# The router's second sum in another PSUM bank, and the normed rows of two latent tiles behind the choice

## The chip, the cores and the metric

The kernel runs on one core of one Trainium2 chip. The time is the device time of one execution in microseconds (us); of several executions the median is taken.

## The reference

Two layers of a transformer-like block over 1024 latent tokens and 256 context tokens of 1024 channels. Each layer mixes tokens with three parallel head groups (latent attention, a convolution module, a Hyena), and then does, for latent and context tokens apart:

```python
y = concat([rmsnorm(att, g_att), rmsnorm(conv, g_conv), rmsnorm(hy, g_hy)])   # 512 + 256 + 256 channels
x = x + g1 * (y @ w_out)
h = rmsnorm(x, norm2_g) * (1 + sc2) + sh2
# expert choice: 16 experts
aff = softmax(h @ router_w)                      # tokens x 16
gates, idx = top_k(aff.T, 2 * n_tokens // 16)    # 128 latent, 32 context tokens for each expert
y = (silu(h[idx] @ w_gate) * (h[idx] @ w_up)) @ w_down
x = x + g2 * scatter_add(idx, y * gates)
```

In layer 1, the last, only latent tokens go through this part. After it comes a final RMSNorm.

## The kernel before

The change lies in the output projection (`wout`) and at the start of the experts (`moe`) that follow it. Before them stand the input projection and the three head groups, behind them sixteen experts for each layer.

`wout(l)` works on tiles of 128 tokens: in layer 0 eight latent tiles (0 to 7) and two of context (8, 9) in the order 0, 1, 2, 3, 8, 9, 4, 5, 6, 7; in layer 1 the tiles 0 to 7. The loop calls `heads(i)` for a tile and then `channels` for the tile two places later in the order. The products use three matmuls for each block (`mm3`, lines 95 to 97: high by high, high by low, low by high).

- `channels(i)` computes the convolution's and the Hyena's share of the projection: 24 matmuls into four banks, which ScalarE (L1129) and VectorE (L1130) empty with the RMSNorm scales of the two groups. For tiles 8 and 9 two of the four products go to the "tp" banks.
- `heads(i)` computes attention's share (24 matmuls into two banks). For each half of 512 channels VectorE scales and adds (L1148), multiplies by the gate (L1149) and adds the residual stream (L1150): this is x(i). ScalarE squares and sums x (L1155), GpSimd makes the RMSNorm factor r of it. TensorE transposes x in two halves into "tp" (L1162), ScalarE copies them (L1163), 16 matmuls with the router's weights give partial logits in a bank "rt"; VectorE copies these (L1169), one further product with `sel` (the router's second sum, `pl2`) adds the parts up, and VectorE reads it into the logits "lg" (L1173). Last come the normed rows of the tile, four VectorE operations (L1181, L1182 twice each) and their write to memory `hd` from SP's queue.
- `scales(...)` makes the RMSNorm factors of the groups: matmuls with a column of ones into the bank "st", a VectorE read (L1105), and two GpSimd operations (L105, L106). Both `heads` and `channels` call it, `channels` before its products, `heads` before its own.

PSUM's eight banks in this stage are tp 2, mm 4, rt 1, st 1. `ps("st")` asks for the next use of such a bank.

After context's second tile, `route_ctx` makes context's choice (through two tiles in the bank "rt", the last one read at L1280). After tile 7, `route` makes the latent choice: softmax, and a chain of VectorE operations that sorts, ending with the copy of L1346. `moe` then loads weights, builds for the first expert the list of context tokens, gathers their rows (`fetch_ctx`, L1409), transposes them (`tokens_ctx`) and multiplies by its weights (`up_ctx`, 64 matmuls into "cx"), and does the same for latent tokens (`fetch`, `tokens`, `up`, matmuls into "acc").

The order of work on each engine's queue is made when the kernel is built: a planner with a timeline simulation takes, among the instructions that are ready, the one with the highest priority. Priority is the order of the program, unless a block raises it (`high_priority(n)`). Each engine then runs its queue in that fixed order.

Of the kernel before, what the change touches and what calls it, by code (L numbers as in the profile page):

```python
# [51 lines left out]
class Kernel:  # L52
# [988 lines left out]
    def wout(self, l, R):  # L1041
# [4 lines left out]
        with ExitStack() as es:  # L1046
# [10 lines left out]
            ps = self.banks(es, tp=2, mm=4, rt=1, st=1) if last else self.banks(es, tp=2, mm=4, rt=1, st=1)  # L1057
# [75 lines left out]
            def heads(i):  # L1133

                s = int(i >= 8)
                c = 128 * i % W
                t, y = T[i], Y[128 * i - c]
                r = scales(y[2], c, (0,))
                x = row()
                if l == 0:  # L1140
                    src = A["x"][128 * i:128 * i + 128] if not s else A["ctx"][128 * (i - 8):128 * (i - 8) + 128]
                else:
                    src = self.stream(0, i)
                nc.sync.dma_start(x, src)
                for c2 in range(2):
                    d = slice(512 * c2, 512 * c2 + 512)
                    p = product(y, 0, c, d)
                    V.scalar_tensor_tensor(t[:, d], p, r, t[:, d], ALU.mult, ALU.add)  # L1148
                    V.tensor_tensor(t[:, d], t[:, d], rows[2, s][:, d], ALU.mult)  # L1149
                    V.tensor_tensor(x[:, d], t[:, d], x[:, d], ALU.add)  # L1150
                nc.sync.dma_start(self.stream(l, i), x)
                h = self.t(PX, [128, 1024], F32, "h2")
                s1 = self.t(PX, [128, 1], F32, "s1")
                r1 = self.t(PX, [128, 1], F32, "r1")
                S.activation(h, x, AF.Square, scale=1.0 / 32, accum_out=s1)  # L1155
                R["normed"] = self.rsqrt(r1, s1)

                hT = self.t(PX, [128, 8, 128], F32, "h2T")
                for b in range(2):
                    p = ps("tp", (128, 4, 128))  # L1160
                    for k in range(4):
                        self.T.transpose(p[:, k, :], x[:, 128 * (4 * b + k):128 * (4 * b + k) + 128], self.ident)  # L1162
                    S.activation(hT[:, 4 * b:4 * b + 4, :], p, AF.Copy)  # L1163
                pl = ps("rt")
                for k in range(8):
                    j = k % 4
                    self.mm(pl[32 * j:32 * j + 32, 0:128], rw[:, k, :], hT[:, k, :], k < 4, k >= 4)
                lp = self.t(PX, [128, 128], F32, "lpart")
                V.tensor_copy(lp, pl[:, 0:128])  # L1169
                pl2 = ps("rt")  # L1170
                self.mm(pl2[:, 0:32], lp, sel)
                e = slice(16 * s, 16 * s + 16)
                V.scalar_tensor_tensor(R["lg"][:, i, :], pl2[:, e], r1, cst[:, e], ALU.mult, ALU.add)  # L1173
                if i == 7:
                    return lambda: normed(i, s, h, x, r1)
                normed(i, s, h, x, r1)

            def normed(i, s, h, x, r1):
                for b in range(2):
                    d = slice(512 * b, 512 * b + 512)  # L1180
                    V.scalar_tensor_tensor(h[:, d], x[:, d], r1, rows[4, s][:, d], ALU.mult, ALU.mult)  # L1181
                    V.tensor_tensor(h[:, d], h[:, d], rows[3, s][:, d], ALU.add)  # L1182
                nc.sync.dma_start(self.hd[l][128 * i:128 * i + 128], h)

            def router():

                n = 1 if last else 2
                rr = self.t(PX, [128, 8, 16], F32, "rr", bufs=1)
                rc = self.t(PX, [128, 2, 2, 8], F32, "rc", bufs=1)
                rs = self.t(PX, [128, 32], F32, "rsum", bufs=1)  # L1190
                nc.sync.dma_start(rr, A["router_w"][l])
                nc.sync.dma_start(sel, A["k_sel"])
                for j, v in enumerate((4, 3)):
                    for s in range(n):
                        nc.sync.dma_start(rc[:, j, s], self.modd[l][v, s].rearrange("(k p) -> p k", p=128))
                if last:
                    G.memset(rw, 0.0)
                    G.memset(rs, 0.0)
                for s in range(n):
                    e = slice(16 * s, 16 * s + 16)  # L1200
                    G.tensor_tensor(rw[:, :, e], rr, rc[:, 0, s].unsqueeze(2).to_broadcast([128, 8, 16]), ALU.mult)
                    tmp = self.t(PX, [128, 8, 16], F32, "rtmp", bufs=1)
                    G.tensor_tensor(tmp, rr, rc[:, 1, s].unsqueeze(2).to_broadcast([128, 8, 16]), ALU.mult)
                    V.tensor_reduce(rs[:, e], tmp.rearrange("p k e -> p e k"), AX.X, ALU.add)
                p = ps("rt")
                self.mm(p[:, 0:32], self.ones[:, 0:1].to_broadcast([128, 128]), rs)
                V.tensor_copy(cst, p[:, 0:32])
# [8 lines left out]
            for s in range(1 if last else 2):  # L1216
                for v in (2, 4, 3):
                    r = self.t(PX, [128, 1024], F32, f"row{v}_{s}", bufs=1)
                    (G if last else nc.sync).dma_start(r, _bc(self.modd[l][v, s], 128))
                    rows[v, s] = r  # L1220
            router()
            order = list(range(8)) if last else [0, 1, 2, 3, 8, 9, 4, 5, 6, 7]
            for n, i in enumerate(order):
                end = heads(i)
                if i == 7:
                    self.route(R, ps, "mm" if last else "tp", row() if last else self.t(PX, [128, 1024], F32, "ro", bufs=1))
                    end()
                if n + 2 < nt:
                    channels(order[n + 2])
                if i == 9:  # L1230
                    ar, wk = (self.t(PX, [16, 256], F32, n, bufs=1) for n in ("arc", "wkc"))
                    self.route_ctx(R, ps, ar, wk)
# [116 lines left out]
    def moe(self, l, R):  # L1349
        nc, A, S, V, G = self.nc, self.A, self.S, self.V, self.G  # L1350
        last = l == 1
        with ExitStack() as es:
# [38 lines left out]
            def fetch_ctx(e):  # L1391
                d = E[e]
                p = ps("dt")
                ohc = self.t(P, [128, 2, 64], F32R, "ohc", bufs=1)
                for q in range(2):
                    V.tensor_tensor(ohc[:, :, 32 * q:32 * q + 32], iota[:, 0:32].unsqueeze(1).to_broadcast([128, 2, 32]),
                                    R["slot"][:, 8:10, e:e + 1].to_broadcast([128, 2, 32]), ALU.is_equal)
                for i in range(2):
                    self.mm(p[0:64, 4:8], ohc[:, i, :], R["rhs"][:, 8 + i, e, :], i == 0, i == 1)
                idc = self.t(P, [64, 1], U32, "idc", bufs=4)  # L1400
                V.tensor_copy(idc, p[0:64, 4:5])
                d["idc2"] = self.t(P, [64, 1], U32, "idc2", bufs=6)
                V.scalar_tensor_tensor(d["idc2"], p[0:64, 4:5], 2.0, half, ALU.mult, ALU.add)
                glc = self.t(P, [64, 2], F32, "glc", bufs=4)
                V.tensor_copy(glc, p[0:64, 6:8])
                d["gatec"] = self.t(P, [64, 1], F32, "gatec", bufs=6)
                G.tensor_tensor(d["gatec"], glc[:, 0:1], glc[:, 1:2], ALU.add)
                d["xgc"] = self.t(P, [32, 1024], F32, "xgc", bufs=1)
                G.indirect_dma_start(d["xgc"], None, self.hd[l], bass.IndirectOffsetOnAxis(ap=idc[0:32, :], axis=0))  # L1409
# [15 lines left out]
            def tokens_ctx(e):  # L1425
                d = E[e]
                d["xc"] = self.t(P, [128, 8, 32], F32, "xcT")
                p = ps("dt")
                for k in range(8):
                    self.T.transpose(p[:, 32 * k:32 * k + 32], d["xgc"].rearrange("p (f k) -> p k f", k=8)[:, k, :], self.ident[0:32, 0:32])  # L1430
                S.activation(d["xc"].rearrange("p a b -> p (a b)"), p[:, 0:256], AF.Copy)
# [40 lines left out]
            def up_ctx(e, kh):  # L1472
                d = E[e]
                if kh == 0:
                    d["pc"] = ps("cx")
                for kk in range(4):
                    k = 4 * kh + kk
                    for m in range(2):
                        for c in range(2):
                            r = 32 * (2 * m + c)  # L1480
                            self.mm(d["pc"][r:r + 32, :], d["xc"][:, k, :], raw(e, m, kh)[:, kk, 512 * c:512 * c + 512], k == 0, k == 7)
# [92 lines left out]
                E[0]["raw"] += [weights(nm, 0, 1) for nm in ("w_gate", "w_up")]  # L1574
            if not last:
                E[0]["raw"] += [weights(nm, 0, 1) for nm in ("w_gate", "w_up")]
                fetch_ctx(0)
                tokens_ctx(0)
                up_ctx(0, 0)
                up_ctx(0, 1)  # L1580
            fetch(0)
            tokens(0)
            for e in range(1, AHEAD):
# [244 lines left out]
```

## Time and profile before

| | before |
|---|---|
| median of three runs | 3397.47 us (3392.35 to 3399.98) |
| the profiled execution's own time | 3397.73 us |
| its span | 3395.9 us |
| its mean granted TensorE clock | 0.954 of full speed |
| TensorE matmul busy | 3123.1 us (92%) |
| TensorE weight load busy (beside matmuls) | 2226.8 us (66%) |
| VectorE busy | 2531.3 us (75%) |
| ScalarE busy | 1690.2 us (50%) |
| GpSimd busy | 1295.2 us (38%) |
| DMA | 660.84 MB, mean 195 GB/s |

The time is the median over executions; the rows further down come from one profiled execution, whose span is what the profiler saw from the first instruction to the last. Busy shares are averages over the whole span, with stages in it that differ. [...]

### The profile page before, as it was taken

How to read it: one execution, taken by the hardware profiler on the slowest of the kernel's cores; microseconds unless marked ns; L12 is line 12 of the kernel's file. 1: busy time of each engine (PE TensorE's matmuls, PEld its weight loads, DVE VectorE, ACT ScalarE, POOL GpSimd, SP SyncE). 2: the span in 40 equal slices, each digit the busy share in tenths (PEclk: the TensorE clock that was granted, in tenths of full speed). 3: DMA queues.
4: the chain of work that ended last, by engine and by line, in shares of the span. 5: the costliest groups of instructions: out<-in, count | busy, mean ns of one | idle time of the engine just before them, and what ended most of it. 6: DMA issues, size and time to landing. Idle time of an engine off the chain costs nothing. (4 is left out here: it accounts for less than half of the span.)

```text
span 3395.9 us, 42767 instructions
## 1 busy us (share of the span) xinstructions
PE 3123.1 (92%) x15607; PEld 2226.8 (66%) x15607; DVE 2531.3 (75%) x3520; ACT 1690.2 (50%) x2447; POOL 1295.2 (38%) x1128
## 2 busy tenths in 40 slices
PE   8898989999999599999999969899998959999996
PEld 2467865666567376666666657656664747888885
DVE  7755698777657677777777656977775769998986
ACT  4315235433443256656565543353434427777775
POOL 4421255754653212112221122565557423433334
PEclk9898989999999799999999979899999969999998
DMA  8881112231253567777777631221233469999994
GB/s 306 323 279 53 38 64 82 54 104 43 73 162 116 209 241 289 278 286 279 290 292 274 225 101 44 81 72 51 69 110 99 149 235 347 378 382 372 382 378 176
DMA packets 142523, 660.84 MB, mean 195 GB/s; under 512 B 24712, under 2 KB 63272, under 8 KB 111593
## 3 DMA queue, kind: packets, MB, share of 16 engines
q1 hardware_dynamic: 117129, 582.89, 45.6%
q0 software_dynamic: 24768, 74.05, 7.9%
q8 instruction: 123, 2.02, 0.2%
q10 hardware_dynamic: 416, 1.18, 0.1%
q14 instruction: 87, 0.71, 0.1%
HBM read 589.28 MB, written 68.78 MB: 194 GB/s over the span
## 5 line engine op out<-in xcount | busy, mean ns | idle before, releaser
L91 DVE TENSOR_TENSOR mwl<-raw,mwh 128x1024 fp32r<-128x1024 f32 x710 | 881.5, 1278 | 217.5 <-ACT mwh L90 207.2
L90 ACT ACTIVATE mwh<-raw 128x1024 fp32r<-128x1024 f32 x768 | 791.8, 1057 | 350.5 <-PE acc L97 118.1
L96 PE MATMUL acc<-mwl,xh 128*128 128x512 f32 x1024 | 405.0, 396 | 0.0
L97 PE MATMUL acc<-mwh,xl 128*128 128x512 f32 x1024 | 403.0, 396 | 0.1
L95 PE MATMUL acc<-mwh,xh 128*128 128x512 f32 x1024 | 373.7, 401 | 6.0 <-ACT xh L90 6.0
L803 POOL TENSOR_TENSOR psum<-psum,pt 128x512 f32<-128x512 f32 x252 | 332.3, 1338 | 66.7 <-ACT pt L788 56.8
L788 ACT ACTIVATE pt<-s 128x512 f32<-128x512 f32 (+1 forms) x336 | 195.9, 586 | 257.4 <-PE s L97 220.8
L1528 POOL DMA_INDIRECT xd<-ymoe,idx x31 | 113.4, 3656 | 541.6 <-DVE ymoe L1524 465.1
L758 DVE TENSOR_REDUCE mx<-p 128x1 f32<-128x512 f32 (+1 forms) x374 | 206.0, 585 | 70.0 <-PE p L100 68.9
L95 PEld LDWEIGHTS acc<-mwh,xh 128*128 128x128 f32 x1024 | 192.4, 189 | 68.6 <-ACT mwh L90 10.9
L96 PEld LDWEIGHTS acc<-mwl,xh 128*128 128x128 f32 x1024 | 193.9, 189 | 40.1 <-DVE mwl L91 0.8
L91 POOL TENSOR_TENSOR mwl<-raw,mwh 128x1024 fp32r<-128x1024 f32 x58 | 150.1, 2592 | 181.3 <-ACT mwh L90 117.5
L97 PEld LDWEIGHTS acc<-mwh,xl 128*128 128x128 f32 x1024 | 192.8, 189 | 39.1 <-DVE xl L91 0.6
L100 PE MATMUL o<-pt,Vt 128*64 128x512 f32 (+1 forms) x672 | 184.7, 613 | 0.0
L564 DVE SCALAR_TENSOR_TENSOR cacc<-pad,cw,cacc 128x1295 f32<-128x1295 f32 (+1 forms) x90 | 165.8, 1842 | 1.3
L97 PE MATMUL mm<-hTh,wfl 128*128 128x512 f32 (+1 forms) x400 | 151.3, 379 | 12.8 <-DVE wfl L91 12.8
L95 PE MATMUL mm<-hTh,wfh 128*128 128x512 f32 (+1 forms) x400 | 152.5, 381 | 4.0 <-ACT wfh L90 4.0
L96 PE MATMUL mm<-hTl,wfh 128*128 128x512 f32 (+1 forms) x400 | 152.0, 380 | 0.0
L562 POOL TENSOR_TENSOR cacc<-cacc,tap 128x1295 f32<-128x1295 f32 (+1 forms) x30 | 97.0, 3233 | 120.7 <-ACT tap L561 118.5
L100 PE MATMUL cx<-raw,xcT 128*32 128x512 f32 x1024 | 123.7, 607 | 0.0
L95 PE MATMUL mm<-woh,yhh 128*128 128x512 f32 x280 | 115.7, 416 | 8.5 <-ACT wt L1129 4.4
L96 PE MATMUL mm<-wol,yhh 128*128 128x512 f32 x280 | 111.9, 400 | 0.1
(546 smaller groups left out, 7228.9 us busy)
## 6 DMA issues: line engine op xcount, KB each, us to landing
raw<-in_w_gate_dram SPq DMA_DIRECT2D x64, 2048.0 KB
raw<-in_w_up_dram SPq DMA_DIRECT2D x64, 2048.0 KB
raw<-in_w_down_dram SPq DMA_DIRECT2D x64, 2048.0 KB
mw<-in_mod_w_dram SPq DMA_DIRECT2D x48, 1024.0 KB
ht<-in_k_C_dram POOLq DMA_DIRECT2D x24, 512.0 KB, 5.1
wfr<-in_w_fm_dram SPq DMA_DIRECT2D x20, 512.0 KB
hd<-h SPq DMA_DIRECT2D x18, 512.0 KB
fw<-in_k_filt_dram POOLq DMA_DIRECT2D x17, 512.0 KB, 5.8
```

Source lines behind the costliest of these rows:

```text
L90: self.S.activation(hi, src, AF.Copy)
L91: (eng or self.V).tensor_tensor(lo, src, hi.bitcast(F32), ALU.subtract)
L95: mm(out, ah, bh, start=first, stop=False, skip_group_check=True)
L96: mm(out, ah, bl, start=False, stop=False, skip_group_check=True)
L97: return mm(out, al, bh, start=False, stop=last, skip_group_check=True)
L100: return self.T.matmul(out, a, b, start=first, stop=last, skip_group_check=True)
L562: G.tensor_tensor(a, a, t, ALU.add)
L564: V.scalar_tensor_tensor(a, x, w2[:, ct, k:k + 1], a, ALU.mult, ALU.add)
L758: V.tensor_reduce(mx[:, q, n:n + 1], p[:, :N], AX.X, ALU.max)
L788: S.activation(pt[:, :N], p[:, :N], AF.Exp, scale=ATT_SCALE)
L803: (V if tail and n > 8 else G).tensor_tensor(sm[:, :N], st.sums[i][:, :N], pt[:, :N], ALU.add)
L1528: G.indirect_dma_start(self.xd[l], bass.IndirectOffsetOnAxis(ap=d["idx"], axis=0), y, None, compute_op=ALU.add)
```

## The change

There are three edits. The router's second sum asks for the bank "st" instead of "rt". The normed rows of tile 6, and not only those of tile 7, come behind the latent choice in the program's order; a list keeps what has to be made there. And in layer 0 the first expert's context work (list and gather, transposes, 64 matmuls) stands in a block of raised priority, so that the planner places it up to 2500 places earlier than the program's order.

```diff
                 V.tensor_copy(lp, pl[:, 0:128])
-                pl2 = ps("rt")
+                pl2 = ps("st")
                 self.mm(pl2[:, 0:32], lp, sel)
                 e = slice(16 * s, 16 * s + 16)
                 V.scalar_tensor_tensor(R["lg"][:, i, :], pl2[:, e], r1, cst[:, e], ALU.mult, ALU.add)
-                if i == 7:
-                    return lambda: normed(i, s, h, x, r1)
-                normed(i, s, h, x, r1)
+                if i in (6, 7):
+
+                    ends.append(lambda: normed(i, s, h, x, r1))
+                else:
+                    normed(i, s, h, x, r1)
...
             router()
+            ends = []
             order = list(range(8)) if last else [0, 1, 2, 3, 8, 9, 4, 5, 6, 7]
             for n, i in enumerate(order):
-                end = heads(i)
+                heads(i)
                 if i == 7:
                     self.route(R, ps, "mm" if last else "tp", row() if last else self.t(PX, [128, 1024], F32, "ro", bufs=1))
-                    end()
+                    for end in ends:
+                        end()
...
             if not last:
                 E[0]["raw"] += [weights(nm, 0, 1) for nm in ("w_gate", "w_up")]
-                fetch_ctx(0)
-                tokens_ctx(0)
-                up_ctx(0, 0)
-                up_ctx(0, 1)
+                with self.tc.high_priority(2500):
+                    fetch_ctx(0)
+                    tokens_ctx(0)
+                    up_ctx(0, 0)
+                    up_ctx(0, 1)
```

## Rows read from the trace of the kernel before

**Rows 1.** Window of layer 0's projection; columns: stretch, length, PE, PEld, DVE, ACT, POOL busy (instructions), granted clock, DMA share, GB/s.

```profile
1000.00:1107.00 107.00, 107.00 (x598) 84.96 (x597) 84.91 (x155) 38.95 (x65) 42.03 (x59) 1.00 0.35 125
```

**Rows 2.** Windows of tile st alone, layer 0 and layer 1; busy columns PE, PEld, DVE, POOL.

```profile
1007.70:1091.00 83.30, 4.67 (x36) 5.87 (x37) 1.79 (x12) 6.79 (x12) 1.00 0.36 127
2662.30:2690.10 27.80, 1.57 (x12) 1.89 (x13) 0.59 (x4) 2.25 (x4) 1.00 0.44 152
```

**Rows 3.** Timeline of tp in layer 0 (start, us, instruction), then the window of tile mm.

```profile
1015.16 0.60 ACT L1163 ACTIVATE h2T<-tp 128x512 f32<-128x512 f32 x1 [0.48 <-PE tp L1162]
...
1027.58 0.60 PE L1162 MATMUL tp<-ident,xres 128*128 128x128 f32 x4
...
1030.56 0.50 PE L95 MATMUL tp<-woh,yhh 128*128 128x512 f32 x1
...
1021.70:1030.50 8.80, 7.82 (x30) 5.16 (x29) 0.84 (x2) 0.00 (x0) 1.00 0.23 73
```

**Rows 4.** Timeline of layer 0's first step: x of tile 0, head products of tile 1.

```profile
997.91 0.69 DVE L1150 TENSOR_TENSOR xres<-wt,xres 128x512 f32<-128x512 f32 x1
...
1001.29 0.48 PE L95 MATMUL mm<-woh,yhh 128*128 128x512 f32 x1
```

**Rows 5.** Timeline of VectorE at layer 1's tile 7, from x to lg.

```profile
2732.85 0.68 DVE L1150 TENSOR_TENSOR xres<-wt,xres 128x512 f32<-128x512 f32 x1
...
2735.74 1.41 DVE L1181 SCALAR_TENSOR_TENSOR h<-xres,r,row 128x512 f32<-128x512 f32 x2 [2.21 <-POOL r L106]
...
2738.47 0.23 DVE L1173 SCALAR_TENSOR_TENSOR lg<-rt,r,cst 128x16 f32<-128x16 f32 x1
```

**Rows 6.** Groups in 1000 to 1107: L105 by tile (ns min/median/max); others by line (count | busy, mean ns | idle).

```profile
L105 POOL TENSOR_SCALAR rst<-st x16: 213/628/1189, 1004.0 to 1104.8; 128x1 f32<-128x1 f32 x9, 128x2 f32<-128x2 f32 x7
...
L106 POOL TENSOR_TENSOR rst<-rst,mhalf 128x1 f32<-128x1 f32 (+1 forms) x16 | 14.3, 896 | 1.2
...
L1148 DVE SCALAR_TENSOR_TENSOR wt<-mm,rst,wt 128x512 f32<-128x512 f32 x17 | 12.7, 749 | 11.2 <-PE mm L97 9.2 <-POOL rst L106 2.0
```

**Rows 7.** Layer 0's tail: window of tile mm at tile 6's head products, and VectorE's timeline.

```profile
1097.70:1103.30 5.60, 5.60 (x24) 4.53 (x25) 1.47 (x2) 0.00 (x0) 1.00 0.25 98
...
1081.47 0.23 DVE L1173 SCALAR_TENSOR_TENSOR lg<-rt,r,cst 128x16 f32<-128x16 f32 x1 [1.37 <-PE rt L100]
...
1108.75 0.18 DVE L1280 COPY slot<-rt 128x32 f32<-128x32 f32 x1
...
1121.63 0.23 DVE L1173 SCALAR_TENSOR_TENSOR lg<-rt,r,cst 128x16 f32<-128x16 f32 x1 [0.73 <-PE rt L100]
```

**Rows 8.** Timeline behind the choice, in layer 0 and then in layer 1.

```profile
1146.37 0.29 DVE L1346 COPY slot<-tp 128x128 f32<-128x128 f32 x1 [0.57 <-PE tp L1345]
...
1148.42 1.04 POOL L1409 DMA_INDIRECT xgc<-hd,idc  x1 [21.29 <-DVE glc L1405]
...
1154.33 9.54 PE L100 MATMUL cx<-raw,xcT 128*32 128x512 f32 x64
...
1171.04 0.79 PE L95 MATMUL acc<-mwh,xh 128*128 128x512 f32 x1
...
2766.93 0.29 DVE L1346 COPY slot<-mm 128x128 f32<-128x128 f32 x1 [0.57 <-PE mm L1345]
...
2777.97 0.80 PE L95 MATMUL acc<-mwh,xh 128*128 128x512 f32 x1
```

**Rows 9.** Windows of all engines where TensorE's clock differs, columns as in the first group.

```profile
1171.00:1181.00 10.00, 10.00 (x46) 8.24 (x46) 6.84 (x14) 4.96 (x6) 3.19 (x4) 0.90 0.19 51
2778.00:2788.00 10.00, 10.00 (x30) 8.17 (x29) 2.69 (x5) 2.93 (x4) 5.91 (x4) 0.52 0.17 52
973.00:977.10 4.10, 0.20 (x3) 0.11 (x2) 3.87 (x5) 1.35 (x4) 3.36 (x3) 0.75 0.70 180
977.00:982.00 5.00, 4.90 (x12) 3.87 (x13) 3.85 (x4) 3.71 (x7) 3.34 (x4) 0.51 1.01 220
987.00:991.00 4.00, 1.39 (x6) 0.85 (x5) 0.54 (x1) 1.72 (x2) 0.00 (x0) 1.00 0.48 72
```

## The prediction

> **What bounds the kernel now.** I read the page first (TensorE busy 92% of the span), then the window of layer 0's output projection, because the change lies there and right behind it. TensorE is busy for every one of its 107.00 us at full clock, VectorE for 84.91 [rows 1]. So this stage loses what TensorE is made to wait, and gains nothing from an engine beside it.
>
> Next the PSUM bank "st", alone. In 83.30 us it serves 12 sums (12 VectorE reads): two a token tile, for six tiles, so a tile takes 13.9 us; layer 1 shows 27.80 us for two tiles, again 13.9 [rows 2]. Four sum matmuls take about 0.52 us, VectorE's read 0.15: the bank is nearly always free.
>
> Then the order in which banks are handed out. A tile of "tp" is freed at 1015.76, and no transpose takes it until 1027.58, tile 2's second half; only behind this comes tile 8's first product in "tp", at 1030.56. All the while products of "mm" ran: 30 matmuls in the window, more than the 24 of one tile's head products [rows 3]. A later request does not overtake an earlier one of the same tag, ready or not. The prediction rests on this.
>
> **The change part by part.** *The router's second sum moves from "rt" to "st".* The requests to "st" ran: scales of heads(i), scales of channels(i+2), scales of heads(i+1). Now the router's sum of tile i stands between the first two. It needs x(i) complete, then transposes, copy, logits, a copy, and is freed by the read "lg". Scales of channels(i+2) queue behind it; without them nothing empties the four "mm" banks that hold channels(i+2); without these, the products of heads(i+1) can't start; and x(i+1) needs those. This makes a loop:
>
> - 24 head matmuls, 5.60 us of window with TensorE full [rows 7];
> - the last half's three VectorE operations, 3 x 0.75 [rows 6] = 2.2;
> - x to lg: in layer 1's last tile x is complete at 2733.53 and lg ends at 2738.70, 5.2 us, of which 1.41 is a normed operation ahead [rows 5] and about 0.5 (estimate) ScalarE's square ahead of the copy; so 3.3 to 5.2;
> - sums 0.5 and read 0.15 [rows 2];
> - GpSimd's two operations, 0.21 to 1.19 and 0.90 [rows 6]: 1.1 to 2.1;
> - emptying the first bank, 0.75, at worst behind another 0.75 [rows 6]; hand-offs between engines 0.5 to 0.7, an estimate beside the 0.57 that VectorE waited behind one matmul [rows 8].
>
> That is 14.1 to 18.0; I take the middle, 16.1, because VectorE, 79% busy, lets queues form but not always. Against 13.9 a step is 2.2 longer (0.2 to 4.1).
>
> The first step is worse: before, heads(1) started at 1001.29, while x(0) was complete at 998.60 [rows 4]. Without products and VectorE's three operations the loop is 6.3 to 10.2, so 1004.9 to 1008.8: +5.5 (3.6 to 7.5).
>
> Layer 0 has eight such steps: the first, five ordinary ones, 5 x 2.2 = 11 (1 to 20.5), and two for channels of context tiles, which hold two "mm" banks instead of four; there two free banks let the head products go on, and I put 0.5 each (0 to 2 each). Layer 1 has the first, 5.5, and five, 11.
>
> *The hold by context's choice.* lg of tile 9 is read at 1081.47, and context's choice leaves "rt" at 1108.93 [rows 7], 27.5 us on. Until then tile 4's logits can't use "rt". Before, four tiles' logits merely piled up and went through in 12.9 us. After, the sums of tile 4 hold "st", so the pipeline stops with them. The same logits are wanted about 14 us behind lg of tile 9; but some of the 27.5 was queueing between head products, which a stalled TensorE doesn't impose. +3 (0 to 13).
>
> *The tail.* From the window in which tile 6's products run, 1097.70, to lg of tile 7, 1121.86, are 24.2 us [rows 7]. The pile is gone after, which saves up to 3.5 of its 12.9 (estimate); but heads(7)'s scales wait for tile 6's lg. -1 (-3.5 to +2.8, two normed operations). In layer 1, with no pile, the same link costs +2 (-0.5 to +5, one x-to-lg).
>
> *Normed rows of tile 6 behind the choice.* Zero: tile 7's were deferred already and still ran in front of its lg (2735.74 before 2738.47, [rows 5]), since the planner fills idle VectorE time. What hides them is that idle time; uncovered, two operations, 2.8, and the write of the rows on SP's queue behind them, with weight loads behind it (rival E).
>
> *Context's first expert, planned ahead.* After layer 0's choice, from its last copy to the first expert product, are 1171.04 - 1146.37 = 24.7 us; in layer 1, without context, 2777.97 - 2766.93 = 11.0 [rows 8]. The gather of context rows sat in GpSimd's queue for 21.29 us and issued at 1148.42, and the 64 context matmuls, 9.54 us, came behind the choice [rows 8]. Done ahead, up to 13.6 go. [...] If layer 0 becomes like layer 1, 10 x (0.90 - 0.52) = 3.8 come back: -10 (-13.6 to -7). The cover is the choice, VectorE work with TensorE mostly idle; without it, up to 9.54 us of context products would stand in TensorE's queue ahead of the choice's own matmuls, and a third of that is the -7. The gather crosses GpSimd's queue, whose later operations are the choice's small casts; SP's transfers don't change order with it.
>
> **Sum.** Layer 0: 5.5 + 11 + 1 + 3 - 1 - 10 = 9.5. Layer 1: 5.5 + 11 + 2 = 18.5. Together +28 on the profiled execution's 3397.73 us (span 3395.9 and 1.8 around it): 3426. The median of the runs, 3397.47, is 0.3 away. All low ends: -12.5 and +4.1, 3389. All high ends: +41 and +33, 3472. Ends so many don't fall together; 3405 to 3450 is this case's own range.
>
> **The rivals.** *B, the clock.* Each stall also slows TensorE. For it: after a stretch with 0.20 us of TensorE work in 4.10, the next 5 us had a granted 0.51, 2.45 us lost; against it: with 1.39 busy in 4.00, so 2.61 idle, the clock stayed 1.00 [rows 9], and my gaps are 2.2. Twelve first and ordinary gaps x 2.45 = 29: 3455. [...]
>
> *C, the other side.* Sums of channels don't queue behind the router's, because the planner hands "st" out by readiness. Then no step stalls, logits no longer share a bank with their sum, and the tails gain 4 (layer 0's pile) and 1.3, the context work 10: 3382. It decides if channels' sums are seen between a tile's scales and its lg. Against it stands the wait for "tp" [rows 3].
>
> *D, the stalls cancel.* Steps at their low ends cost 3.6 + 1 in each layer, tail and hold nothing, the context work gains 10: about 3397, no difference.
>
> *E, the rows come late.* The first expert's gather waits for rows of tiles 6 and 7 in memory, now both behind the choice: tile 6's four operations, twice 1.41 and two like them [rows 5], go uncovered, 5.6 at most, 5 in each layer on top of the forecast: 3436.
>
> [...]
>
> **How the numbers follow.** My forecast 0.55, B 0.15, C 0.10, D 0.12, E 0.08. The likeliest is 3426. From 3398 to 3462 lie the forecast's own range and its nearer tails, E, most of B and half of D; what is left out is C, D's other half and B with long steps. A difference under 0.2%, 6.8 us, can't be told from none. Faster by more: C and the lowest corner, 0.11. Within: D, 0.11. Slower: 0.78.
>
> **What would show it.** In the window of layer 0's projection TensorE is no longer full: a gap of 1 to 4 us a tile, ended by emptying an "mm" bank or by the scales, just behind an lg. Twelve "st" reads become eighteen, in the order scales, lg, scales; tiles come every 15 to 17 us. lg follows x by 3 to 5 us instead of a step later. The context matmuls lie inside the choice, and expert products start some 11 to 14 us behind its last copy. Layer 1 is 12 to 25 us longer up to its choice. The prediction is wrong if channels' sums run ahead of lg, if x to lg falls under 3 (then the loop hides in 13.9), or if context products delay the choice.

## The result and the profile after

The changed kernel takes 3495.4 us (median of six runs, 3488.27 to 3500.59) against 3396.19 before: a ratio of 1.0288, 95% interval 1.0274 to 1.0302. It is slower by 99 us. The direction was forecast; the forecast was +28 us, with a range that ended at 3462.

First the windows of layer 0's projection, as in [rows 1], of six tiles from lg to lg in layer 1 (five steps), and of one tile's stretches; the columns are those of the first group.

```profile
1000.00:1107.00 107.00, 90.83 (x433) 70.25 (x432) 56.56 (x98) 31.28 (x50) 24.31 (x43) 0.86 0.34 113
...
2712.60:2813.90 101.30, 85.63 (x400) 65.36 (x400) 51.15 (x95) 28.24 (x57) 21.56 (x45) 0.83 0.31 104
...
2750.50:2753.00 2.50, 0.98 (x13) 0.52 (x11) 1.46 (x4) 0.60 (x1) 0.00 (x0) 1.00 0.55 100
2753.00:2755.50 2.50, 1.13 (x6) 0.96 (x6) 0.32 (x2) 0.60 (x2) 1.58 (x3) 0.62 0.81 320
2755.50:2758.00 2.50, 2.36 (x6) 1.88 (x7) 1.41 (x2) 1.80 (x5) 1.96 (x5) 0.50 0.00 0
2758.00:2760.50 2.50, 2.50 (x8) 1.93 (x7) 0.00 (x0) 0.00 (x0) 0.00 (x0) 0.51 0.00 0
2760.50:2763.00 2.50, 2.50 (x12) 2.05 (x11) 1.95 (x3) 0.00 (x0) 0.00 (x0) 1.00 0.00 0
2755.64:2763.62 7.98, 7.98 (x26) 6.35 (x27) 3.53 (x5) 1.85 (x5) 1.82 (x4) 0.70 0.00 0
```

TensorE was full in this stage, and now is busy for 91 of 107 us, at a mean granted clock of 0.86. Five tiles take 101.3 us, so a tile takes 20.3 us instead of 13.9 [rows 2]. Of these 20.3, TensorE is busy for 17.1 (it did the same products in 13.9): half of the 6.4 lost is waiting, the other half is products that take longer. The head products, which run in part at a granted 0.50, account for 2.4 of that half: 7.98 us instead of 5.60 [rows 7].

Now one tile in the timeline of VectorE, TensorE and ScalarE in turn, layer 1, in the order of time within each engine.

```profile
2743.43 0.75 DVE L1148 SCALAR_TENSOR_TENSOR wt<-mm,rst,wt 128x512 f32<-128x512 f32 x1 [0.45 <-PE mm L97]
2744.09 0.68 DVE L91 TENSOR_TENSOR yll<-yin,yhh 128x512 fp32r<-128x512 f32 x1
...
2745.97 0.68 DVE L1150 TENSOR_TENSOR xres<-wt,xres 128x512 f32<-128x512 f32 x1
...
2752.59 0.23 DVE L1173 SCALAR_TENSOR_TENSOR lg<-st,r,cst 128x16 f32<-128x16 f32 x1 [0.50 <-PE st L100]
2753.58 0.16 DVE L1105 TENSOR_SCALAR st<-st 128x2 f32<-128x2 f32 x1 [0.76 <-PE st L100]
...
2749.68 0.51 PE L97 MATMUL mm<-woh,yll 128*128 128x512 f32 x1
2750.02 0.60 PE L1162 MATMUL tp<-ident,xres 128*128 128x128 f32 x4
2751.30 0.43 PE L100 MATMUL rt<-h2T,rw 128*32 128x128 f32 x8 [0.69 <-ACT h2T L1163]
2752.14 0.41 PE L100 MATMUL st<-sel,lpart 128*128 128x32 f32 x2 [0.41 <-DVE lpart L1169]
2752.97 0.58 PE L100 MATMUL st<-ones,ysq 128*128 128x1 f32 x4 [0.42 <-DVE lg L1173]
2753.80 0.59 PE L100 MATMUL st<-ones,ysq 128*128 128x1 f32 x2 [0.25 <-DVE st L1105]
2755.64 0.79 PE L95 MATMUL mm<-woh,yhh 128*128 128x512 f32 x1 [1.26 <-ACT wt L1129]
...
2754.90 1.27 ACT L1129 ACTIVATE wt<-mm,rst 128x512 f32<-128x512 f32 x2 [3.65 <-POOL rst L106]
```

The forecast loop stands there link by link. The sums of channels wait for VectorE's read lg (0.42 us, released by lg); VectorE's read of the sums, GpSimd and ScalarE follow; TensorE's next head products are released by ScalarE's emptying of a bank. Then x, and round again.

The end of layer 0's tail and what comes behind its choice, from the same trace:

```profile
1004.67 0.69 DVE L1150 TENSOR_TENSOR xres<-wt,xres 128x512 f32<-128x512 f32 x1
...
1179.67 0.23 DVE L1173 SCALAR_TENSOR_TENSOR lg<-st,r,cst 128x16 f32<-128x16 f32 x1
...
1203.91 0.35 DVE L1400 TENSOR_TENSOR ohc<-iota,slot 128x64 fp32r<-128x64 f32 x2
1204.56 0.29 DVE L1350 COPY slot<-tp 128x128 f32<-128x128 f32 x1 [0.30 <-PE tp L1349]
...
1206.46 1.04 POOL L1413 DMA_INDIRECT xgc<-hd,idc  x1 [21.28 <-DVE glc L1409]
...
1212.33 9.67 PE L100 MATMUL cx<-raw,xcT 128*32 128x512 f32 x64
...
1229.18 0.79 PE L95 MATMUL acc<-mwh,xh 128*128 128x512 f32 x1
...
2883.72 0.80 PE L95 MATMUL acc<-mwh,xh 128*128 128x512 f32 x1
```

The spans differ by 3496.7 - 3395.9 = 100.8 us. Up to layer 0's first expert product it is 1229.18 - 1171.04 = 58.1; from there to layer 1's, 1654.5 against 1606.9 [rows 8], 47.6; behind it -4.9, in work that the change doesn't touch. Of the 58.1, 6.8 lie ahead of the loop: x of tile 0 is complete at 1005.36 instead of 998.60, behind work that the change doesn't touch either (executions of the kernel before differ by up to 7.6 us among themselves). Within layer 0, x of tile 0 to lg of tile 7 grew from 123.3 [rows 4, 7] to 174.5, +51 (in layer 1 from 93.3 to 136.8, +44); lg of tile 7 to the first expert product was 49.2 and is 49.3. The context work gained nothing: its list instruction moved ahead of the choice's last copy, but the gather still issues 1.9 us behind it (before, 2.05), and the 64 products follow.

### The profile page after: what moved, and what is told of

Read it like the earlier page. It is cut to its first block, busy times and chain, and to the rows that moved or that the text cites. A ratio compares the mean times of both kernels' runs of the same rounds, so it can differ in the third digit from the quotient of the medians.

```text
span 3496.7 us, 42723 instructions
## 1 busy us (share of the span) xinstructions
PE 3172.1 (91%) x15607; PEld 2258.1 (65%) x15607; DVE 2532.3 (72%) x3520; ACT 1692.2 (48%) x2447; POOL 1271.2 (36%) x1128
## 5 line engine op out<-in xcount | busy, mean ns | idle before, releaser
L91 DVE TENSOR_TENSOR mwl<-raw,mwh 128x1024 fp32r<-128x1024 f32 x710 | 882.7, 1280 | 211.7 <-ACT mwh L90 202.2
L91 POOL TENSOR_TENSOR mwl<-raw,mwh 128x1024 fp32r<-128x1024 f32 x58 | 149.9, 2589 | 177.5 <-ACT mwh L90 117.5
L95 PE MATMUL mm<-woh,yhh 128*128 128x512 f32 x280 | 128.8, 463 | 28.6 <-ACT wt L1129 19.2
L96 PE MATMUL mm<-wol,yhh 128*128 128x512 f32 x280 | 124.5, 445 | 0.5 <-DVE wol L1074 0.5
```

The lines of the kernel that those rows point to most:

```text
L91: (eng or self.V).tensor_tensor(lo, src, hi.bitcast(F32), ALU.subtract)
L95: mm(out, ah, bh, start=first, stop=False, skip_group_check=True)
L96: mm(out, ah, bl, start=False, stop=False, skip_group_check=True)
```

## The experiments

Each run's ratio is to the kernel before on the same chip, with its 95% interval. A tag is the name, such as "st", under which the kernel asks for a bank.

**The bank alone, and the rest alone.** `st_alone` has only `pl2 = ps("st")`; `rest_alone` has everything else.

> Only the router's second sum moves to the bank st; the normed rows and the context's first expert stay as before. Theory 1 (channels' sums queue behind the logits' read in st, and TensorE waits for emptied banks): the whole loss is here, 3485 to 3505 us, lg to lg some 20 us a tile in layer 1 as in the changed kernel (20.3), against 13.9 before. Theory 2 (the other two edits change the planned order and bring the loss): 3390 to 3410.

> The other two edits without the move of the bank: normed rows of tile 6 behind the choice, context's first expert at raised priority. Theory 1: 3390 to 3402, no difference; the two list instructions of context go ahead of the choice's last copy, the gather and the 64 products do not, so from that copy to the first expert product it stays at 24 to 26 us. My prediction's term of -10 us would give 3386. Theory 2: 3480 or more.

Measured: 3497.5 us, 1.0283 (1.0266 to 1.0301), and 3398.45 us, 0.9997 (0.9987 to 1.0008). The whole loss is the bank. The deferral and the raised priority together do nothing that can be measured, so my -10 us is refuted, and theory 2 with it.

**What in the bank: order or number.** The first attempt asks for the sums of channels ahead of the second sum; the second gives st another bank, at the cost of one of mm.

```diff
+                if nxt is not None:
+                    n = 128 * nxt
...
+                    SC[nxt] = scales(Y[n - n % W][2], n % W, (1, 2))
                 pl2 = ps("st")
...
-            ps = self.banks(es, tp=2, mm=4, rt=1, st=1) if last else self.banks(es, tp=2, mm=4, rt=1, st=1)
+            ps = self.banks(es, tp=2, mm=3, rt=1, st=2) if last else self.banks(es, tp=2, mm=3, rt=1, st=2)
```

> All three edits, but the sums of channels (tile two places on) are asked for in the program just ahead of the router's second sum of the tile, so they stand in front of it in the queue for st. The bank, its users and their number are those of the changed kernel. Theory 1: the loop is cut, tiles come every 14 to 15 us again, 3393 to 3410. Rival (the loss comes from the second sum sharing a bank at all, or from the router's work in TensorE's queue): 3470 to 3500.

> All three edits, with two banks for st and three instead of four for mm. Theory 1: a sum of channels takes the bank that the scales of heads have left while the router's sum holds the other, so most of the loss goes: 3395 to 3435, the upper end if three mm banks cost something of their own. Rival (one mm bank less costs as much as it frees): 3450 to 3500.

Measured: 3474.18 us, 1.0214 (1.0196 to 1.0232), and 3499.43 us, 1.0302 (1.0283 to 1.0322). Both expectations missed, and both times fell where the rivals had put them. In the first, the loop had only moved: some 18 us a tile. VectorE's timeline there:

```profile
2741.61 0.23 DVE L1178 SCALAR_TENSOR_TENSOR lg<-st,r,cst 128x16 f32<-128x16 f32 x1
2743.39 0.16 DVE L1105 TENSOR_SCALAR st<-st 128x1 f32<-128x1 f32 x1 [1.55 <-PE st L100]
...
2746.67 1.41 DVE L1148 SCALAR_TENSOR_TENSOR wt<-mm,rst,wt 128x512 f32<-128x512 f32 x2 [1.66 <-POOL rst L106]
```

The single sum behind lg is that of the next tile's heads, now the one that stands behind the second sum; without it VectorE can't finish x of the next tile. In the second run, TensorE's timeline:

```profile
2746.99 0.41 PE L100 MATMUL st<-sel,lpart 128*128 128x32 f32 x2 [0.78 <-DVE lpart L1169]
2747.23 1.04 PE L100 MATMUL st<-ones,ysq 128*128 128x1 f32 x6
```

The six sum matmuls follow the second sum at once, and VectorE's lg comes only at 2747.45: they don't wait for the read any more, but they still wait until the earlier request of the tag has begun, which is what [rows 3] had shown for "tp". A second bank saves the wait for the read and leaves the wait for x.

**The order shown.** With the same eight banks as the run before, the second sum gets a tag of its own; and with one bank st, the next heads' sums are asked for ahead of it too, beside those of channels.

```diff
-            ps = self.banks(es, tp=2, mm=4, rt=1, st=1) if last else self.banks(es, tp=2, mm=4, rt=1, st=1)
+            ps = self.banks(es, tp=2, mm=3, rt=1, st=1, sel=1) if last else self.banks(es, tp=2, mm=3, rt=1, st=1, sel=1)
...
-                pl2 = ps("st")
+                pl2 = ps("sel")
...
+                if after is not None:
+                    n = 128 * after
+                    HS[after] = scales(Y[n - n % W][2], n % W, (0,))
```

> All three edits, three banks for mm as in the run with two st banks, but the eighth bank has a tag of its own that only the router's second sum asks for. The two runs differ in the tag alone. Theory 1 as the last runs sharpen it (what counts is the order of requests within a tag: a request waits until the earlier one has begun, even with a bank free): channels' sums no longer stand behind the second sum, tiles come every 14 to 15.5 us, 3393 to 3425. Rival (three mm banks are the bound there): 3480 to 3505 as with two st banks.

> All three edits, one bank st as in the changed kernel; the sums of channels two places on and those of the next tile's heads are both asked for ahead of the router's second sum. In the run with channels' sums alone ahead, the next heads' sums stood behind the second sum and gave a loop of 18.6 us a tile. Theory 1: no sum that a tile needs soon stands behind the second sum, 14 to 15.5 us a tile, 3393 to 3420. Rival (any sharing of st with the second sum costs): 3455 or more.

Measured: 3407.6 us, 1.0019 (1.0008 to 1.0030), and 3425.52 us, 1.0075 (1.0052 to 1.0098). The tag alone is worth 1.0302 - 1.0019 of the time, some 96 us, with the same eight banks; what is left, 0.2%, may come from three mm banks instead of four, which no run tests by itself. The window of layer 1's tiles, with its own tag, four steps:

```profile
2660.40:2718.30 57.90, 55.72 (x315) 42.82 (x314) 40.02 (x75) 20.89 (x44) 19.67 (x31) 1.00 0.40 137
```

A tile takes 14.5 us, and the clock stays at 1.00. Asking for both sums first gives back three quarters of the loss on the very bank of the changed kernel; 25 us stay, a little above the range that I gave; their cause is open.

**TensorE's order.** In the changed kernel the second transposes of x stand behind all 24 products of channels. Two variants put 12 of these later: behind the transposes (TR holds the tile's last one; this is the edit shown), or behind channels' sums (TR holds the last of these, and the tiles from the third on are meant).

```diff
-                    pg = [product(y, g, c, d, "tp" if i >= 8 and g == 1 else "mm") for g in (1, 2)]
+                    with self.tc.issue_after(TR[-1].ins) if c2 and TR else ExitStack():
+                        pg = [product(y, g, c, d, "tp" if i >= 8 and g == 1 else "mm") for g in (1, 2)]
```

> All three edits; in TensorE's queue the second half of channels' products is put behind the second transposes of x, which the planner had placed behind all 24 products. Theory: x to lg falls from 6.2 us to 4 or 4.5, and 12 products fill TensorE while it waits for the logits, so a tile falls from 20.3 to 16 to 18 us: 3430 to 3470. Rival (TensorE's order does not matter, the wait for the bank alone sets the tile): 3485 to 3500.

> All three edits; the second 12 of channels' products come in TensorE's queue behind the sums of channels, so the transposes, the logits and the second sum go right behind x, and the 12 products fill the wait between sums and emptied banks. Theory (the loop through st sets the tile, and in the changed kernel two things stretch it: the router's work behind products in TensorE's queue, and the lower clock): x to lg 3.3 to 4, and head products 5.6 + VectorE 3.2 + x to lg 3.3 to 4 + sums 0.5 + 12 products 2.8 = 15.4 to 16.1 a tile at full clock: 3410 to 3440. Rival (sharing the bank costs more than the loop says): 3460 or more.

Measured: 3490.84 us, 1.0267 (1.0247 to 1.0287), and 3497.39 us, 1.0293 (1.0278 to 1.0309). Both missed, and fell where the rivals had put them. In the first, the 12 products merely moved from ahead of the transposes to ahead of the last logits, and x to lg was still 5.7 us, of 6.2. In the second, x to lg fell to 5.1 us and the wait was filled, but the loop stayed at 20.2. Its windows, from x to the sums, of the 12 products, and of the 24:

```profile
2745.90:2751.90 6.00, 2.89 (x28) 1.92 (x26) 2.96 (x6) 1.73 (x3) 0.78 (x2) 0.83 0.60 187
2751.90:2757.10 5.20, 5.20 (x15) 4.15 (x16) 0.91 (x2) 1.37 (x2) 0.95 (x2) 0.54 0.40 159
2757.10:2762.80 5.70, 5.70 (x29) 4.71 (x28) 2.95 (x5) 1.53 (x4) 2.63 (x5) 1.00 0.00 0
```

Behind 6 us in which TensorE was busy for 2.9, the 12 products run at a granted 0.54 and take 5.2 us; the next 24 take 5.7 at 1.00. The loss at the lower clock is about as large as before, some 2.4 us (5.2 instead of half of 5.6), and has only moved from the head products to these 12, which now stand on the loop.

**The clock by itself.** Unused work of TensorE, whose results nothing reads and which does no part of the computation, was put into the waits. First in the wait behind channels' sums, eight products and then four:

```diff
+                if n == 2:
+                    w = ps("rt")
+                    for _ in range(8):
+                        self.mm(w[0:2, 0:128], st, sq3[:, 0, c:c + 128])
```

> All three edits, and behind each read of channels' sums eight further 128x128 products into the bank rt, whose result nothing reads, in the wait of about 2 us before TensorE's next products. They do no part of the computation. Theory of the clock: of the 6.4 us that a tile lost, 3.2 are TensorE's products at the lower clock (17.1 us busy a tile for work that took 13.9), the filled wait keeps the clock up, and 12 to 14 tiles gain 2 to 3 us each: 3450 to 3475. Rival (the fall of the clock starts in the earlier waits, or costs nothing): 3488 to 3505.

> As the filled wait, with four unused products instead of eight. With eight the head products fell from 7.98 to 6.58 us, but began about 1 us late behind them. Theory of the clock: four end in time and keep part of the gain, 3470 to 3485. Rival (less filling, less clock): 3485 to 3500.

Measured: 3487.31 us, 1.0260 (1.0234 to 1.0285), and 3491.48 us, 1.0273 (1.0257 to 1.0288). Neither is told apart from the changed kernel (1.0274 to 1.0302); the first lies between the two ranges, the second in the rival's. With eight, the head products of a tile fell from 7.98 us at 0.70 to 6.58 at 0.86:

```profile
2748.64:2755.22 6.58, 6.58 (x27) 5.34 (x28) 2.95 (x5) 1.55 (x4) 2.61 (x5) 0.86 0.00 0
```

But they began at 2748.64, 1.1 us after ScalarE had emptied the first bank (VectorE's operation behind that starts at 2747.56), since the fillers were still running. The rival was right in one point: the fall starts in the earlier waits. Here the grant is 0.81 over the 2.50 us from 2745.5 to 2748.0 and 0.50 over the next 2.50, although the fillers keep TensorE busy from 2745.84 to 2748.27. So the waits ahead of the logits were filled as well, on top of the half-filled wait and on top of the order with the sums first: four transposes behind the second transposes, and behind the logits 8 products in the one and 16 in the other.

```diff
+                w = ps("tp", (128, 4, 128))
+                for k in range(4):
+                    self.T.transpose(w[:, k, :], x[:, 128 * (4 + k):128 * (4 + k) + 128], self.ident)
...
+                w = ps("tp")
+                for k in range(16):
+                    self.mm(w[0:32, 0:128], rw[:, 4 + k % 4, :], hT[:, 4 + k % 4, :])
```

> As the half-filled wait, and in addition four unused transposes behind the second transposes of x and eight unused logit products behind the logits, in the waits for ScalarE's and VectorE's copies; nothing reads their results. Theory of the clock (2.4 us of a tile's 20.3 are head products at a granted 0.70 instead of 1.00, because TensorE waits before them): the head products go to 5.6 to 6.3 us, a tile to 18 to 19, 3455 to 3475. Rival (the clock falls whatever fills the waits, or the fillers delay as much as they save): 3485 to 3500.

> The kernel whose 12 products follow the sums (20.3 us a tile; these 12 took 5.2 us at a granted 0.54), with four unused transposes and sixteen unused logit products in the waits between x and the logits. Theory of the clock: the 12 products take 2.8 us, a tile 17.8 to 18.5, 3455 to 3470, against 3497 without them. Rival: 3490 to 3500.

Measured: 3494.31 us, 1.0280 (1.0263 to 1.0297), and 3496.49 us, 1.0280 (1.0262 to 1.0297). Both fell into the rivals' ranges; the first rival had said that the fillers may delay as much as they save. The clock rose as expected, to 0.97 and 1.00 over 100 us of layer 1, and in the second the 12 products took 2.98 us instead of 5.20; but its sixteen fillers ran 3.66 us in a wait of 1.46, and the second sum came 1.95 us late. Of this second run, a window of 100 us, that of one tile's 12 products, and the fillers:

```profile
2707.00:2807.00 100.00, 95.91 (x612) 78.51 (x610) 51.41 (x99) 30.09 (x59) 22.72 (x47) 1.00 0.29 100
...
2766.62:2769.60 2.98, 2.98 (x17) 2.49 (x16) 0.91 (x2) 1.27 (x2) 0.95 (x2) 1.00 0.56 224
...
2761.77 3.66 PE L100 MATMUL tp<-h2T,rw 128*32 128x128 f32 x32
```

So with fewer, 5 and 2:

> As the filled version before it, with five unused logit products instead of sixteen: the sixteen kept the clock at 1.00 but ran 3.66 us in a wait of 1.46, so the second sum came 1.95 us late in every tile of 18.9. Theory of the clock: five take 1.15 us and delay nothing, the clock stays at 1.00, a tile takes 17.0: 3450 to 3470. Rival (the clock falls again with fewer): 3485 to 3500.

> As all waits filled, with two unused logit products instead of eight, which ran 1.91 us in a wait of 0.65. Theory of the clock: the second sum comes 1.2 us earlier in a tile, head products take 5.6 to 6.6 us, a tile 18 to 18.6: 3460 to 3478. Rival (less work in the waits, and the clock falls): 3485 to 3500.

Measured: 3477.94 us, 1.0236 (1.0216 to 1.0256), and 3483.57 us, 1.0249 (1.0226 to 1.0273); both a little above the ranges of the theory and below those of the rival. In the first, tiles of 17.7 and of 19.3 us alternate. The windows of the 12 products in two neighbouring tiles:

```profile
2771.99:2775.00 3.01, 3.01 (x17) 2.50 (x16) 0.91 (x2) 1.27 (x2) 0.95 (x2) 1.00 0.64 261
2752.72:2756.97 4.25, 4.25 (x16) 3.40 (x15) 0.91 (x2) 1.27 (x2) 0.95 (x2) 0.67 0.54 209
```

Work that computes nothing makes the kernel with the sums first 19 us faster (3478 against 3497; the intervals of the ratios don't touch), and a tile is short where the clock stays at 1.00. So the lower clock is a cause and no companion: 20.3 us a tile without fillers, 17.7 where they hold the clock. It is not the whole: 17.7 is still 3.8 more than the 13.9 of before.

**The stretch behind the choice.** On the kernel before, the first expert's context list, gather and transposes were given memory of their own in a pool that is open already, and two banks of the projection, at raised priority; and in another run the six low parts of its weights, which GpSimd made in front of the latent gather, went to VectorE. `first_ctx` is what `fetch_ctx(0)` and `tokens_ctx(0)` do, traced behind the normed rows of tile 7.

```diff
+                    if not last:
+                        with self.tc.high_priority(2500):
+                            self.first_ctx(l, R, ps)
...
-                fetch_ctx(0)
-                tokens_ctx(0)
+                E[0].update(R["ctx0"])
...
-                product(raw(e, m, kh), kh, d["x"], d["acc"][m], (4, 2)[m] if e == 0 and kh == 0 else 0)
+                product(raw(e, m, kh), kh, d["x"], d["acc"][m], (4, 2)[m] if last and e == 0 and kh == 0 else 0)
```

> The kernel before, and only the context rows of layer 0's first expert gathered and transposed ahead: list, rows and transposes get memory of their own and banks of the projection, so they are no part of the expert stage's pools, and stand at raised priority. No bank of the router and no normed rows are moved. Theory (in the changed kernel the raised priority moved nothing because the planner opens the expert stage's pools only when the projection's last tiles are read): the gather runs during or before the choice, the 64 context products start right behind it, and from the choice's last copy to the first expert product 24.7 us become 13 to 18: 3384 to 3393. Rival (the latent gather or the weights' split is what this stretch waits for): 3394 to 3400.

> The kernel before, with the low parts of the first expert's weights in layer 0 (six operations) made by VectorE instead of GpSimd. In the run with the early gather the choice's own VectorE operations took 1.3 to 2.4 us instead of 0.3 to 0.4 while GpSimd made these low parts, and in the kernel before they stand in GpSimd's queue ahead of the latent gather (11.62 us). Theory: without them the gather issues at about 7 us from the choice's last copy instead of 15, VectorE's list operation takes 1.2 us instead of 7.75, and the first expert product comes 4 to 8 us earlier: 3389 to 3394. Rival (VectorE's queue then holds the list up just as long): 3396 to 3401.

Measured: 3410.68 us, 1.0034 (1.0022 to 1.0046), and 3398.23 us, 1.0002 (0.9993 to 1.0011). Both missed: the first lies above both of its ranges, the second in its rival's. The early gather did go ahead, and the 64 products stood right behind the choice (1155.30). But GpSimd's low parts now began inside the choice (five of them from 1145.23 on, 11.83 us), and its VectorE chain ran slower, so that its last copy came at 1155.41 instead of 1146.37, and the first expert product at 1175.04. Of these differences 2.1 us lie ahead of the choice (lg of tile 7 at 1123.71 instead of 1121.63); the choice itself, from lg to the copy, took 31.7 us instead of 24.7. VectorE in that run, and the same operations in the kernel before:

```profile
1147.76 2.33 DVE L1366 TENSOR_TENSOR ro<-ro 128x128 f32<-128x128 f32 x1
...
1150.12 2.44 DVE L1367 TENSOR_TENSOR_SCAN ro<-ro 128x128 f32<-128x128 f32 x1
```

```profile
1144.67 0.29 DVE L1337 TENSOR_TENSOR ro<-ro 128x128 f32<-128x128 f32 x1
...
1144.99 0.43 DVE L1338 TENSOR_TENSOR_SCAN ro<-ro 128x128 f32<-128x128 f32 x1
```

That run's total of +13 us is not explained by this stretch, which starts its experts only some 4 us later; where the rest arises is open. In the last run it is the other way round: GpSimd's gather took 7.83 us, while VectorE's six low parts took 6.88 us from 1149.64 on:

```profile
1149.61 7.83 POOL L1409 DMA_INDIRECT xgc<-hd,idc  x1 [23.60 <-DVE glc L1405]
```

## Why the prediction was wrong

The mechanism was right, and the runs show it. Requests of one tag are served in order; channels' sums stand behind the router's second sum; TensorE waits each tile for a bank that they would empty. `st_alone` holds the whole loss, and `own_tag` takes nearly all of it away with the tag alone. Rival C, sums by readiness, is refuted.

**The term that was mis-sized is the loop, "14.1 to 18.0; I take the middle, 16.1".** A tile takes 20.3 us; above what was before, 6.4 instead of 2.2. By its links in layer 1's tile:

| link | predicted | measured |
|---|---|---|
| head products | 5.6 | 7.98 |
| VectorE's last half | 2.2 | 3.2 |
| x to lg | 3.3 to 5.2, about 4.25 | 6.2 |
| lg to the next product | the rest, about 4.05 | 2.8 |
| a tile | 16.1 | 20.2 |

- *Head products.* I took 5.60 us from a stage in which TensorE never waits, and put the clock apart as rival B, on the ground that a gap of 2.61 us had stayed at 1.00 [rows 9] and mine was 2.2. The loop has not one gap but a row of short ones: behind lg of one tile TensorE is released five times within 5 us and is busy for 2.1 of 2750.5 to 2755.5; the grant falls inside this stretch and is 0.50 from 2754.0 to 2760.0. B was no rival but a link of the forecast; the filled runs show that it is a cause. Its price, 2.45 us a step, was close to the 2.4 by which the head products grew, but B added to the forecast came to 3455 only: the next two links were set too low as well.
- *x to lg.* My ends came from layer 1's last tile [rows 5], where no channels' products are left. In every other tile the second transposes stand behind 24 of them: x is complete at 2746.65, they start at 2750.02. The planner had put them there, and the order of work in TensorE's queue belongs to the loop. How much this order costs is not shown: the two runs that changed it took 0.5 and 1.1 us off x to lg, and neither shortened the tile clearly.
- *VectorE's last half.* Three operations that split the next source tile (L91, one of them in the lines above) stand between the three, so they take 3.2 us and not 2.2.

The other terms. *The two context steps*, 0.5 each because they hold two mm banks: wrong, layer 0's ten tiles take 18.4 to 21.3 us from x to x, but for the last. *The hold by context's choice*, +3: nothing; its last read comes 14 us behind lg of tile 9 instead of 27.5, and lg of tile 4 another 6 us later, at the loop's own pace. VectorE is less crowded there (56.6 us of 107 instead of 84.9); that this is the reason was not tested. *The tail*: not told apart from the loop. *The normed rows*, zero: right, by `rest_alone`. *The context work*, -10: wrong in its first half, the work did not move. The raised priority carried only the list instruction ahead of the choice's last copy. That the planner opens the expert stage's pools only behind the projection's last reads agrees with the early gather, which went ahead once it had memory of an open pool; the rule itself was not tested further. And the second half would have failed too: there the work moved, and gained nothing. The 3.8 us in this term, 10 x (0.90 - 0.52) from the granted clocks of [rows 9], no run shows: in the changed kernel the first 10 us of expert products ran at 0.90 in layer 0 again, behind the context products, and at 0.68 in layer 1.

With 6.4 us instead of 2.2, taken for all ten, the ordinary steps cost 64 instead of 22; with the first steps, 7.0 and 5.7 (forecast 5.5 each), and the two context steps, some 6 each, this is most of the 95 us that the two stages grew, and no -10 stands against it. Rivals D and E did not come: no gain cancelled the stalls, and the first expert started no later behind the choice.

## What to carry to other kernels

Before a short-lived result is given a bank that "is nearly always free", write down the order of requests for it: what the next request needs counts, and whether the earlier one can begin soon, not how long the bank is held; here a second bank under the same tag did not help (1.0302), a tag of its own did (1.0019). When a loop on the path gets longer than TensorE's work, cost its links with the queues as the planner orders them, and cost the products at the lower clock as part of the loop (here 7.98 us at a granted 0.70 instead of 5.60 at 1.00). A raised priority is no move until the order of instructions shows it.

## What had not been expected of the hardware

- TensorE's clock fell to a granted 0.50 behind a series of short waits (in the tile shown 0.69, 0.41, 0.42 and 0.25 us), and rose again 3.4 or 6.8 us later within the same tile, in layer 0 from its first tile to its eighth and in layer 1 from its second to its seventh; unused work in those waits held it at 1.00 over 100 us of layer 1, or at 1.00 for the 12 products of one tile and 0.67 for those of its neighbour, and made the kernel with the sums first 19 us shorter where it did not itself delay.
- VectorE and GpSimd held each other up here. While GpSimd made low parts of 128x1024 (five in 11.83 us, 2.37 each), VectorE's operations of 0.29 and 0.43 us took 2.33 and 2.44, about the time of one low part; while VectorE made them (six in 6.88 us), GpSimd took 7.83 us to issue a gather that otherwise took 1.04, a little more than the time of all six. In the changed kernel the same VectorE operation (L1381, 128x1024) took 1.22 us at 1204.89, with GpSimd idle, and 7.80 at 1212.60, while GpSimd made four such low parts (9.31 us from 1209.99 on). The cause was not shown. So work that is moved from one of the two to the other didn't leave its neighbour alone here.
